# Every second MLP weight chunk split into two parts by DMA instead of by VectorE

## The chip, the cores and the metric

The kernel runs on one core of a Trainium2 chip. The metric is the device time of one execution in microseconds (us); less is better. A core has five engines with instruction queues of their own: TensorE (PE, with its weight loads PEld), VectorE (DVE), ScalarE (ACT), GpSimd (POOL) and SyncE (SP). They meet only at semaphores. DMA transfers are issued from the queues of SP, ACT and POOL and move data between DRAM and the on-chip memory SBUF on 16 DMA engines.

## What is computed

One decoder layer for 256 tokens of width 1024. The input is normalised and projected; attention and a gated recurrence run side by side, are merged and projected back; then comes an MLP. The part that the change touches is the MLP's weights:

```
u = rms_norm(h, mlp_pre_norm[l])
m = jnp.square(jax.nn.relu(u @ w_mlp_up[l])) @ w_mlp_down[l]
h = h + rms_norm(m, mlp_post_norm[l])
```

All products are wanted at nearly float32 accuracy. TensorE works here on a shorter format, float32r, so each float32 operand is split as hi = round(raw) and lo = raw - hi, and each product is made of three: hi by hi, hi by lo, lo by hi.

## The kernel before

All weights lie in DRAM as 74 chunks of 1 MB, each a tile of 128 partitions x 2048 float32, in their order of use. Chunks 0 to 41 belong to the mixer, 42 and 43 to the MLP's first 512 up-projected columns, 44 to 57 (C_UP) to the rest of the up projection, 58 to 73 (C_DN) to the down projection.

For each chunk `load` (L65) takes a buffer `wraw` and lets SP issue the transfer. `split` (L75) then lets ScalarE round the raw tile into `whi` (L89), and VectorE subtract to get `wlo` (L90). For chunks 17 to 22 VectorE does the rounding too (L87). Each of the three kinds of tile has three buffers (L45 to L47), which are reused: a load waits until the split has read the raw buffer, and a split waits until TensorE has finished with the chunk that had its buffers.

`ahead(c)` (L95) is called before and after the products with a chunk and keeps loads three to four chunks and splits one to two chunks in front of the products. Splits are recorded at high priority, so a scheduler moves them forward among the other work of their engine; it also decides which buffer a tile gets. After that each engine runs its instructions strictly in order.

In the up projection (L596 to L616) a chunk takes 16 pairs of matrix products: 512 columns with `whi` (L606), then 256 columns with `wlo` (L607). ScalarE and VectorE then square the result and split it (L608 to L616). In the down projection (L470 to L483, products at L465 to L467) a chunk takes products with `whi`, `wlo` and `whi` again. In both, the second kind of product already needs `wlo`.

At the start, SP issues the input pieces, then chunks 1 and 2 in quarters and 3 in halves (L119 to L121), then the tokens `x_tok` (L124), then the later chunks. ScalarE's sums of squares over `x_tok` (L219) stand ahead of the rounding of chunk 4 in its queue.

Of the kernel before, what the change touches and what calls it, by code (L numbers as in the profile page):

```python
# [9 lines left out]
F32 = mybir.dt.float32  # L10
F32R = mybir.dt.float32r
AF = mybir.ActivationFunctionType
ALU = mybir.AluOpType
PSUM = bass.MemoryType.PSUM

P = 128
T = 256
D = 1024
# [4 lines left out]
MASK_VALUE = -1e30  # L23

# chunks of weights, 1 MB each, in their order of use
# (x_lru and v in turns)
C_XL, C_V, C_Q, C_K, C_RGA, C_RGI = 0, 1, 8, 12, 16, 17
C_GL, C_GA, C_GEL, C_BA, C_BL, C_OUT, C_UPT, C_UP, C_DN = 18, 22, 26, 30, 34, 38, 42, 44, 58
NCHUNK = 74

# the part of a chunk whose upper half is taken by the vector engine instead of the scalar engine
HI_ON_VECTOR = {c: 1.0 for c in range(17, 23)}

# columns of the channel-major parameters (8 columns each)
(P_W0, P_W1, P_W2, P_W3, P_CB, P_BA, P_BI, P_LAM, P_G1, P_G2) = range(0, 80, 8)
# [4 lines left out]
def hybrid_layer(ctx: ExitStack, tc: tile.TileContext, head_d, x_d, w_d, cst_d, gp_d, out_d):  # L40
    nc = tc.nc

    const = ctx.enter_context(tc.tile_pool(name="const", bufs=1))
    slot = ctx.enter_context(tc.tile_pool(name="slot", bufs=1))
    wraw_p = ctx.enter_context(tc.tile_pool(name="wraw", bufs=3))  # L45
    whi_p = ctx.enter_context(tc.tile_pool(name="whi", bufs=3))
    wlo_p = ctx.enter_context(tc.tile_pool(name="wlo", bufs=3))  # L47
# [13 lines left out]

# [1 line left out]
    raws, splits = {}, {}  # L63

    def load(c, parts=1):  # L65
        raw = wraw_p.tile([P, 2048], F32, tag="wraw", name=f"wraw{c}")
        n = 2048 // parts
        for i in range(parts):
            nc.sync.dma_start(raw[:, i * n:(i + 1) * n], w_d[c - 1, :, i * n:(i + 1) * n])
        raws[c] = (raw, parts)  # L70

    # chunks whose parts stay longer lie in tiles that are free by then
    own_slots = {C_OUT + 2: (8, 10), C_OUT + 3: (5, 6)}

    def split(c):  # L75
        raw, parts = raws.pop(c)
        if c in own_slots:
            hi, lo = (slot_tile(i, f"w{c}_{i}", F32R, (P, 2048)) for i in own_slots[c])
        else:
            hi = whi_p.tile([P, 2048], F32R, tag="whi", name=f"whi{c}")  # L80
            lo = wlo_p.tile([P, 2048], F32R, tag="wlo", name=f"wlo{c}")
        n = 2048 // parts
        for i in range(parts):
            s = slice(i * n, (i + 1) * n)
            k = i * n + int(n * HI_ON_VECTOR.get(c, 0))
            if k > i * n:
                nc.vector.tensor_copy(hi[:, i * n:k], raw[:, i * n:k])  # L87
            if k < (i + 1) * n:
                nc.scalar.copy(hi[:, k:(i + 1) * n], raw[:, k:(i + 1) * n])  # L89
            nc.vector.tensor_tensor(lo[:, s], raw[:, s], hi[:, s].bitcast(F32), ALU.subtract)  # L90
        splits[c] = (hi, lo)
# [3 lines left out]
    def ahead(c):  # L95
        """loads and splits that run ahead of the products with chunk c"""
        while state["load"] < min(NCHUNK, c + 4):
            load(state["load"])
            state["load"] += 1
        while state["split"] < min(NCHUNK, c + 2):  # L100
            with tc.high_priority():
                split(state["split"])
            state["split"] += 1

# [1 line left out]
    eps = const.tile([P, 1], F32, name="eps")  # L106
    nc.vector.memset(eps, EPS)
    first = small.tile([P, 1], F32, tag="warm", name="first")
    nc.scalar.copy(first, eps)
    # parameters, then by block of the contraction: x, features on partitions, and chunk 0 of the weights  # L110
    head = const.tile([P, NPAR + 512], F32, name="head")
# [14 lines left out]
    make_identity(nc, ident)  # L126
    # mask[q, 128 + k] = k <= q ? 0 : MASK_VALUE
    mask = const.tile([P, 2 * P], F32, name="mask")
# [21 lines left out]

# [1 line left out]
    def three(out, wh, wl, xh, xl, start, stop):  # L152
# [4 lines left out]
    def first_chunk(xh, xl):  # L157
        """the same, block by block of the contraction, as the operands arrive"""
        hi, lo = splits.pop(0)
        banks = [mm_bank(f"mm0_{o}")[:, 0:T] for o in range(2)]  # L160
        for kb in range(KB):
            for o in range(2):
                s = slice(kb * 256 + o * P, kb * 256 + (o + 1) * P)
                three(banks[o], hi[:, s], lo[:, s], xh[:, kb, :], xl[:, kb, :], kb == 0, kb == KB - 1)
        return banks

    def feat_chunk(c, xh, xl, urgent=False):
        """two blocks of output features, [P features, 2, T]; unless what follows is urgent, the next split precedes it"""
        ahead(c + 1)
        hi, lo = splits.pop(c)  # L170
        hi = hi.rearrange("p (k c) -> p k c", k=KB)
        lo = lo.rearrange("p (k c) -> p k c", k=KB)
        bank = mm_bank(f"mm{c}").rearrange("p (o t) -> p o t", o=2)
        for o in range(2):
            for kb in range(KB):
                s = slice(o * P, (o + 1) * P)
                three(bank[:, o, :], hi[:, kb, s], lo[:, kb, s], xh[:, kb, :], xl[:, kb, :],
                      kb == 0, kb == KB - 1)
        if not urgent:
            ahead(c + 2)  # L180
        return bank

    # x_lru and the causal convolution
    PADW = T + 4
# [4 lines left out]
    xcl = slot_tile(6, "xcl", F32R)  # L189
    # v, tokens on partitions  # L190
    vt = slot.tile([P, 2, D], F32, tag="s11", name="vt")
# [61 lines left out]

    # sp8 = 8 softplus(-lam) = 8 (max(-lam, 0) + log1p(exp(-|lam|))), log1p(z) = 2 atanh(z / (2 + z))
    lam = par[:, P_LAM:P_LAM + 8]
# [23 lines left out]

    # q, k with rotary positions on features 0..31 of each head  # L280
    # (rows 0..31 of all heads are brought together as [4 x 32, 2 heads, T] for it)
    swap = list(range(16, 32)) + list(range(16))
# [19 lines left out]

    # r, i gates
    rt = slot_tile(7, "rt")
# [16 lines left out]

    # RG-LRU: a = exp(-sp8 r), mult^2 = -expm1(-2 sp8 r) = tanh(sp8 r) (1 + a^2)
    mult = slot_tile(3, "mult")
# [25 lines left out]

    # attention, one head in steps  # L350
    ath = slot_tile(12, "ath", F32R)
# [34 lines left out]
    heads = []  # L386
# [8 lines left out]

    # the three gates, with the attention of one head between chunks
    gL = slot_tile(4, "gL")
# [28 lines left out]

    # branch projections; merged = 0.5 (1 + tanh(gL / 2)) y_lru + 0.5 (1 + tanh(gA / 2)) y_attn
    mgh = slot_tile(1, "mgh", F32R)
# [18 lines left out]

# [1 line left out]
    halves = (slice(0, 512), slice(512, 1024))  # L449

    def tok_products(c0, n, act, parts):
        """act(kb) -> (hi, lo) of [P, T]; the last two chunks go one part of the result at a time"""
        acc = [[at_bank(f"acc{c0}_{b}{i}") if i < 2 else mm_bank(f"acc{c0}_{b}{i}") for i in range(len(parts[b]))]
# [31 lines left out]
    class TokenNorm:  # L485
        """1 / sqrt(mean(y^2) + eps) per token, y in parts"""

# [18 lines left out]

    # output projection, post norm, residual; then the next norm's input, features on partitions
    # (both parts of a block side by side, [P, T upper | T lower])
    u2 = [slot_tile(i, f"u2_{i}", F32R, (P, 4, 512)) for i in (12, 3)]
# [36 lines left out]
    def square_of_norm(b):  # L546
        """the norm's factor enters relu(.)^2 as its square, per token, after the down projection"""
        n = TokenNorm("h", 2)
        for i in range(2):
            r2 = n.part(i, x_tok[:, b, halves[i]])  # L550
        nc.vector.tensor_tensor(scl2[:, b:b + 1], r2, r2, ALU.mult)
# [5 lines left out]

# [1 line left out]
    rrh = [slot_tile(i, f"rrh{i}", F32R) for i in (4, 1, 2, 5)]  # L559
    rrl = [slot_tile(i, f"rrl{i}", F32R) for i in (7, 6, 8, 10)]  # L560

    # the first 512 columns with tokens on partitions, one block of tokens at a time
    ahead(C_UPT + 1)
# [69 lines left out]
def _rotary(np):  # L633
    """cosines and signed sines for rows 0..31 of a head, four times over"""
    inv = np.float32(500000.0) ** (-np.arange(0, 32, 2, dtype=np.float32) / np.float32(32))
    ang = (np.arange(T, dtype=np.float32)[:, None] * inv[None, :].astype(np.float32)).T
    cos = np.concatenate([np.cos(ang)] * 2)
    sin = np.concatenate([-np.sin(ang), np.sin(ang)])
    return np.tile(np.stack([cos, sin], axis=1), (4, 1, 1)).astype(np.float32)


def _pack(np, inp):
    """layout only: pieces of the inputs in the order and the form in which the chip reads them"""
    def a(name):
# [70 lines left out]
```

## Time and profile before

| | |
|---|---|
| time, median of 2 runs | 449.38 us (449.33 to 449.43) |
| span of the profiled execution | 447.7 us |
| PE busy | 437.3 us (98%) |
| DVE busy | 302.2 us (67%) |
| ACT busy | 241.0 us (54%) |
| POOL busy | 21.5 us (5%) |
| DMA moved | 83.59 MB, mean 187 GB/s |

The span is what the profiler saw of one execution; the time is 1.7 us longer. A busy share is over the whole span, so it says nothing on which engine ends a given stage; that is read from the waits and from the order in time.

### The profile page before, as it was taken

How to read it: one execution, taken by the hardware profiler on the slowest of the kernel's cores; microseconds unless marked ns; L12 is line 12 of the kernel's file. 1: busy time of each engine (PE TensorE's matmuls, PEld its weight loads, DVE VectorE, ACT ScalarE, POOL GpSimd, SP SyncE). 2: the span in 40 equal slices, each digit the busy share in tenths (PEclk: the TensorE clock that was granted, in tenths of full speed). 3: DMA queues.
4: the chain of work that ended last, by engine and by line, in shares of the span. 5: the costliest groups of instructions: out<-in, count | busy, mean ns of one | idle time of the engine just before them, and what ended most of it. 6: DMA issues, size and time to landing. Idle time of an engine off the chain costs nothing.

```text
span 447.7 us, 7026 instructions
## 1 busy us (share of the span) xinstructions
PE 437.3 (98%) x2916; PEld 402.2 (90%) x2916; DVE 302.2 (67%) x383; ACT 241.0 (54%) x342; POOL 21.5 (5%) x48
## 2 busy tenths in 40 slices
PE   6999999999999999999999999999999999999994
PEld 6999999999999999999998878888888888888884
DVE  5749975779997666885688566777777744444425
ACT  6686743409897575553556475555555433333322
POOL 1000073202000000000000000000000000000000
PEclk9999999999999999999999999999999999999999
DMA  8977555655634356355567703455555545455202
GB/s 269 408 286 284 180 204 206 215 202 194 208 122 167 122 194 233 120 182 189 187 219 258 277 0 132 171 190 184 192 182 188 188 182 192 184 188 193 83 1 94
DMA packets 14575, 83.59 MB, mean 187 GB/s; under 512 B 1808, under 2 KB 2576, under 8 KB 5456
## 3 DMA queue, kind: packets, MB, share of 16 engines
q1 hardware_dynamic: 13520, 80.39, 49.9%
q0 software_dynamic: 736, 2.36, 1.5%
q8 instruction: 23, 0.38, 0.3%
q10 hardware_dynamic: 288, 0.39, 0.2%
q14 instruction: 8, 0.07, 0.0%
HBM read 81.04 MB, written 1.05 MB: 183 GB/s over the span
## 4 chain that ended last, share of the span: by engine, by line
PE 97%; DMA 1%; ACT 0%; DVE 0%; issue 0%; DVEq 0%; ACTq 0%
PE mm L153 14%; PE mm L154 14%; PE mm L155 14%; PE up L606 12%; PE acc L467 8%; PE acc L466 8%; PE acc L465 8%; PE up L607 6%; PE v L204 2%; PE v L203 2%; PE v L202 2%; PE up L574 1%; PE up L572 1%; PE rg L153 1%; PE rg L155 1%; PE rg L154 1%
## 5 line engine op out<-in xcount | busy, mean ns | idle before, releaser
L90 DVE TENSOR_TENSOR wlo<-wraw,whi 128x2048 fp32r<-128x2048 f32 (+2 forms) x78 | 163.6, 2100 | 89.5 <-ACT whi L89 89.3
L89 ACT CAST whi<-wraw 128x2048 fp32r<-128x2048 f32 (+2 forms) x72 | 125.3, 1740 | 127.8 <-PE acc L467 44.4
L153 PE MATMUL mm<-xgh,whi 128*128 128x256 f32 x384 | 109.8, 290 | 4.2 <-ACT xgh L144 4.2
L154 PE MATMUL mm<-xgl,whi 128*128 128x256 f32 x384 | 109.1, 284 | 0.0
L155 PE MATMUL mm<-xgh,wlo 128*128 128x256 f32 x384 | 108.9, 284 | 0.0
L606 PE MATMUL up<-u,whi 128*128 128x512 f32 x224 | 78.9, 396 | 0.0
L153 PEld LDWEIGHTS mm<-xgh,whi 128*128 128x128 f32 x384 | 72.7, 191 | 4.6 <-ACT xgh L144 4.2
L154 PEld LDWEIGHTS mm<-xgl,whi 128*128 128x128 f32 x384 | 73.4, 191 | 0.5
L155 PEld LDWEIGHTS mm<-xgh,wlo 128*128 128x128 f32 x384 | 73.4, 191 | 0.0
L607 PE MATMUL up<-u,wlo 128*128 128x256 f32 x224 | 63.0, 281 | 0.0
L467 PE MATMUL acc<-whi,rrl 128*128 128x512 f32 (+1 forms) x160 | 56.0, 350 | 0.0
L466 PE MATMUL acc<-wlo,rrh 128*128 128x512 f32 (+1 forms) x160 | 55.8, 349 | 0.0
L465 PE MATMUL acc<-whi,rrh 128*128 128x512 f32 (+1 forms) x160 | 55.7, 348 | 0.0
L606 PEld LDWEIGHTS up<-u,whi 128*128 128x128 f32 x224 | 42.1, 188 | 9.9
L607 PEld LDWEIGHTS up<-u,wlo 128*128 128x128 f32 x224 | 42.3, 189 | 0.0
L466 PEld LDWEIGHTS acc<-wlo,rrh 128*128 128x128 f32 x160 | 30.1, 188 | 4.4
L465 PEld LDWEIGHTS acc<-whi,rrh 128*128 128x128 f32 x160 | 30.2, 189 | 4.3
L467 PEld LDWEIGHTS acc<-whi,rrl 128*128 128x128 f32 x160 | 30.1, 188 | 4.1
L153 PE MATMUL mm<-lrh,whi 128*128 128x256 f32 x64 | 18.1, 283 | 0.0
L154 PE MATMUL mm<-lrl,whi 128*128 128x256 f32 x64 | 18.1, 283 | 0.0
L155 PE MATMUL mm<-lrh,wlo 128*128 128x256 f32 x64 | 18.1, 283 | 0.0
L154 PE MATMUL mm<-atl,whi 128*128 128x256 f32 x64 | 18.0, 282 | 0.0
(197 smaller groups left out, 640.8 us busy)
## 6 DMA issues: line engine op xcount, KB each, us to landing
wraw<-in_w_dram SPq DMA_DIRECT2D x70, 1024.0 KB, 4.8
wraw<-in_w_dram SPq DMA_DIRECT2D x8, 256.0 KB, 6.5
xw_a<-in_head_dram SPq DMA_DIRECT2D x4, 256.0 KB, 3.9
wraw<-in_w_dram SPq DMA_DIRECT2D x2, 512.0 KB, 7.0
x_tok<-in_x_dram SPq DMA_DIRECT2D x1, 1024.0 KB, 9.2
gp<-in_gp_dram POOLq DMA_DIRECT2D x1, 1024.0 KB, 4.6
xw_b<-in_head_dram SPq DMA_DIRECT2D x3, 256.0 KB, 4.6
out_dram<-res ACTq DMA_DIRECT2D x2, 192.0 KB, 2.0
```

The lines of the kernel that those rows point to most:

```text
L89: nc.scalar.copy(hi[:, k:(i + 1) * n], raw[:, k:(i + 1) * n])
L90: nc.vector.tensor_tensor(lo[:, s], raw[:, s], hi[:, s].bitcast(F32), ALU.subtract)
L153: nc.tensor.matmul(out, wh, xh, start=start, stop=False)
L154: nc.tensor.matmul(out, wh, xl, start=False, stop=False)
L155: nc.tensor.matmul(out, wl, xh, start=False, stop=stop)
L202: nc.tensor.matmul(banks[b], xgh[:, kb, s], hi[:, k, :], start=kb == 0, stop=False)
L203: nc.tensor.matmul(banks[b], xgh[:, kb, s], lo[:, k, :], start=False, stop=False)
L465: nc.tensor.matmul(out, xh[:, s], hi[:, hs], start=first, stop=False)
L466: nc.tensor.matmul(out, xh[:, s], lo[:, hs], start=False, stop=False)
L467: nc.tensor.matmul(out, xl[:, s], hi[:, hs], start=False, stop=last)
L606: nc.tensor.matmul(bank, hi[:, kb, c], u2[kb // 4][:, kb % 4, :], start=kb == 0, stop=False)
L607: nc.tensor.matmul(bank[:, 0:T], lo[:, kb, c], u2h(kb, slice(0, T)), start=False, stop=kb == KB - 1)
```

## The change

In the MLP's chunks 44, 46, ... 72 (every second one, 15 in all) neither SP loads a raw tile nor VectorE subtracts. Instead POOL issues two transfers for each:

1. `load`: a transfer from DRAM, float32, straight into a `whi` tile of type float32r. The transfer rounds.
2. `split`: ScalarE writes -hi into the `wlo` tile (an activation with scale -1, in place of the rounding); then POOL issues a second transfer of the same 1 MB, which adds the raw weights to what lies in `wlo`.

The odd chunks stay as they were. The `wraw` tiles have two buffers now instead of three, `whi` four instead of three, for the whole kernel. Comments and docstrings went as well, which shifts line numbers.

```diff
-    wraw_p = ctx.enter_context(tc.tile_pool(name="wraw", bufs=3))
-    whi_p = ctx.enter_context(tc.tile_pool(name="whi", bufs=3))
+    wraw_p = ctx.enter_context(tc.tile_pool(name="wraw", bufs=2))
+    whi_p = ctx.enter_context(tc.tile_pool(name="whi", bufs=4))
...
+    BY_DMA = set(range(C_UP, NCHUNK, 2))
+
     def load(c, parts=1):
+        if c in BY_DMA:
+            hi = whi_p.tile([P, 2048], F32R, tag="whi", name=f"whi{c}")
+            nc.gpsimd.dma_start(hi, w_d[c - 1])
+            raws[c] = (hi, 0)
+            return
...
     def split(c):
         raw, parts = raws.pop(c)
+        if c in BY_DMA:
+            lo = wlo_p.tile([P, 2048], F32R, tag="wlo", name=f"wlo{c}")
+            nc.scalar.activation(lo, raw.bitcast(F32), AF.Copy, scale=-1.0)
+            nc.gpsimd.dma_start(lo, w_d[c - 1], accum_op=ALU.add)
+            splits[c] = (raw, lo)
+            return
```

POOL's queue in the MLP was empty before; its last row was the transfer of the gains `gp`. Now it holds this (`whi54` is chunk 54's rounded tile, L71 the rounding load, L88 the adding load):

```order
L88 DMA wlo50_3169<-in_w_dram 128x2048
L71 DMA whi54_3264<-in_w_dram 128x2048
L88 DMA wlo52_3266<-in_w_dram 128x2048
L71 DMA whi56_3361<-in_w_dram 128x2048
L88 DMA wlo54_3363<-in_w_dram 128x2048
```

So the adding load of chunk 52 stands behind the rounding load of chunk 54, and so on in pairs. By the semaphores in the built program, the load of `whi54` waits for TensorE's last product with chunk 49, whose buffer it takes; the pattern holds from there to the end, `whi` of c + 4 after the products of c - 1.

ScalarE's queue at the same place, before (`rl` is the up projection's copy at L608, `rrh` the rounded activation at L615):

```order
L89 CAST whi53_3319<-wraw53_3219 128x2048
L615 CAST rrh1_2833<-rv_3226 128x512
L608 COPY rl_3274<-up_6_1_3295 128x256
L608 COPY rl_3323<-up_7_0_3325 128x256
L89 CAST whi54_3368<-wraw54_3268 128x2048
```

and now:

```order
L103 CAST whi53_3314<-wraw53_3215 128x2048
L622 COPY rl_3269<-up_6_1_3290 128x256
L622 COPY rl_3318<-up_7_0_3320 128x256
L629 CAST rrh2_2834<-rv_3270 128x512
L87 ACTIVATE wlo54_3363<-whi54_3264 128x2048
```

The negation stands where the rounding of the even chunk stood, with the small `rrh` now ahead of it. It waits for its `whi` to land and for the last product with chunk 51, whose `wlo` buffer it takes.

VectorE's queue early in the kernel, where only the number of raw buffers changed, before (`xc` and `xlp` belong to the convolution, `mm4` is the result of chunk 4's products):

```order
L90 TENSOR_TENSOR wlo5_328<-wraw5_218,whi5_327 128x2048
L246 SCALAR_TENSOR_TENSOR xc_160<-xlp_158,head_86,xc_160 128x256 x2
L90 TENSOR_TENSOR wlo6_397<-wraw6_270,whi6_396 128x2048
L246 SCALAR_TENSOR_TENSOR xc_160<-xlp_158,head_86,xc_160 128x256 x3
L90 TENSOR_TENSOR wlo7_452<-wraw7_325,whi7_451 128x2048
```

and now:

```order
L104 TENSOR_TENSOR wlo5_328<-wraw5_218,whi5_327 128x2048
L260 SCALAR_TENSOR_TENSOR xc_160<-xlp_158,head_86,xc_160 128x256 x6
L255 TENSOR_TENSOR xlp_158<-mm2_276,rstd_365 128x2x256
L255 TENSOR_TENSOR xlp_158<-mm4_400,rstd_365 128x2x256
L104 TENSOR_TENSOR wlo6_397<-wraw6_270,whi6_396 128x2048
```

The subtraction for chunk 6 has moved behind the use of chunk 4's result. On SP, chunk 3's load now waits for the split of chunk 1, and the load of `x_tok` stands behind it as before; chunk 4's load waits for the split of chunk 2 instead of that of chunk 1.

## Rows read from the trace of the kernel before

**Rows 1.** The page, parts 1 and 4: busy time, and the chain that ended last.

```profile
PE 437.3 (98%) x2916; PEld 402.2 (90%) x2916; DVE 302.2 (67%) x383; ACT 241.0 (54%) x342; POOL 21.5 (5%) x48
...
PE 97%; DMA 1%; ACT 0%; DVE 0%; issue 0%; DVEq 0%; ACTq 0%
```

**Rows 2.** Windows, mostly the up projection: busy us per engine, clock, DMA share, GB/s.

```profile
265.00:360.00 95.00, 94.93 (x531) 81.96 (x530) 67.37 (x84) 52.65 (x71) 0.00 (x0) 1.00 0.50 176
```

**Rows 3.** Timeline, up projection: start us, us, instruction, idle before and its releaser.

```profile
318.23 1.91 ACT L89 CAST whi<-wraw 128x2048 fp32r<-128x2048 f32 x1 [2.36 <-PE up L606]
...
320.18 2.29 DVE L90 TENSOR_TENSOR wlo<-wraw,whi 128x2048 fp32r<-128x2048 f32 x1 [1.47 <-ACT whi L89]
...
322.50 5.96 SPq L69 DMA_DIRECT2D wraw<-in_w_dram  x2
...
323.65 0.68 DVE L614 SCALAR_TENSOR_TENSOR rv<-rl 128x512 f32<-128x512 f32 x1
...
323.86 1.91 ACT L89 CAST whi<-wraw 128x2048 fp32r<-128x2048 f32 x1 [2.36 <-PE up L606]
```

**Rows 4.** Timeline, down projection.

```profile
380.17 1.91 ACT L89 CAST whi<-wraw 128x2048 fp32r<-128x2048 f32 x1 [3.71 <-PE acc L467]
...
385.79 1.91 ACT L89 CAST whi<-wraw 128x2048 fp32r<-128x2048 f32 x1 [3.71 <-PE acc L467]
```

**Rows 5.** Windows of 1 us across the load issued at 322.50.

```profile
323.40:324.40 1.00, 1.00 (x8) 0.87 (x7) 0.93 (x3) 0.54 (x1) 0.00 (x0) 1.00 0.80 180
324.40:325.40 1.00, 1.00 (x8) 0.86 (x7) 0.00 (x0) 1.00 (x1) 0.00 (x0) 1.00 0.97 393
325.40:326.40 1.00, 1.00 (x7) 0.91 (x6) 0.60 (x1) 1.00 (x3) 0.00 (x0) 1.00 0.96 401
326.40:327.40 1.00, 1.00 (x7) 0.88 (x6) 1.00 (x1) 0.53 (x2) 0.00 (x0) 1.00 0.18 74
```

**Rows 6.** DMA issues: tile, queue, count, KB each, median us from issue to landing.

```profile
wraw<-in_w_dram SPq DMA_DIRECT2D x70, 1024.0 KB, 4.8
...
gp<-in_gp_dram POOLq DMA_DIRECT2D x1, 1024.0 KB, 4.6
```

**Rows 7.** The issue of `gp` on POOL: ns, start us.

```profile
L446 POOL DMA_DIRECT2D gp<-in_gp_dram x1: 550/550/550, 165.8 to 165.8; - x1
```

**Rows 8.** Windows: `gp` and a load from SP in flight together.

```profile
166.00:167.00 1.00, 1.00 (x11) 1.00 (x10) 0.93 (x1) 1.00 (x4) 0.40 (x1) 1.00 0.00 0
167.00:168.00 1.00, 1.00 (x11) 1.00 (x10) 1.00 (x1) 0.20 (x1) 0.00 (x0) 1.00 0.92 377
...
167.20:172.40 5.20, 5.20 (x45) 5.15 (x44) 2.87 (x7) 2.89 (x8) 0.00 (x0) 1.00 0.98 380
```

**Rows 9.** Timeline where the up projection begins.

```profile
272.94 1.91 ACT L89 CAST whi<-wraw 128x2048 fp32r<-128x2048 f32 x1 [0.89 <-PE up L574]
274.75 0.59 ACT L576 ACTIVATE upt<-up 128x512 f32<-128x512 f32 x1
...
278.69 0.48 PE L606 MATMUL up<-u,whi 128*128 128x512 f32 x1
```

**Rows 10.** Timeline of the start: SP's issues, chunk 4's split, its first product with `wlo`.

```profile
11.98 0.38 SPq L124 DMA_DIRECT2D x_tok<-in_x_dram  x1
...
14.03 7.23 SPq L69 DMA_DIRECT2D wraw<-in_w_dram  x3
...
21.16 1.06 ACT L219 ACTIVATE junk<-x_tok 128x1024 f32<-128x1024 f32 x1 [1.51 <-DMA x_tok<-in_x_dram]
...
25.25 1.91 ACT L89 CAST whi<-wraw 128x2048 fp32r<-128x2048 f32 x1 [0.16 <-DMA wraw<-in_w_dram]
...
27.20 2.29 DVE L90 TENSOR_TENSOR wlo<-wraw,whi 128x2048 fp32r<-128x2048 f32 x1 [1.90 <-ACT whi L89]
...
29.95 0.28 PE L155 MATMUL mm<-xgh,wlo 128*128 128x256 f32 x1
```

**Rows 11.** DMA throughput from 8 to 26 us in 40 slices.

```profile
GB/s 214 137 209 259 341 396 387 392 364 405 428 423 369 382 405 419 401 410 419 410 391 410 419 419 410 428 401 492 401 437 382 401 437 346 492 346 510 364 455 419
```

## The prediction

> **What bounds the kernel now.** I read the busy shares and the chain of work that ended last [rows 1]: TensorE is busy 437.3 of 447.7 us, and 97% of the chain is its own work. So it waits for almost nothing, and the 10.4 us in which it is idle lie at the start and behind the last product. In the stage that the change touches first it is full as well (94.93 of 95 us), while VectorE and ScalarE have room and the DMA engines are half busy [rows 2]. Work taken from VectorE therefore buys nothing; what is left to find is whether the new way of making `wlo` is in time.
>
> For that I read the order in time. ScalarE's roundings of `whi` begin when TensorE releases a buffer, at 318.23 and 323.86 [rows 3], in the down projection at 380.17 and 385.79 [rows 4]: TensorE takes 5.63 us per chunk, 11.26 per pair. Rounding takes 1.91 us and the subtraction 2.29, back to back, so `wlo` is there 4.3 us after the release (320.18 + 2.29 - 318.23 = 4.24). The release is the end of the products with chunk c - 1, and `wlo` of c + 2 is used after those with c and c + 1, 11.26 us later. The old way has 7 us to spare. The new way must fit its two transfers into the same 11.26 us.
>
> **What the change takes away.** 15 subtractions of 2.29 us on VectorE, 34 us: worth nothing, since no wait of TensorE hangs on them. 15 plain loads from SP. On ScalarE the negation takes the place of the rounding; the same tile and the same kind of operation, so 1.91 us each, no change.
>
> **What it adds, timed from s, the end of the products with chunk c - 1 (c even).** By the order, the rounding load of c + 4 and the negation for c + 2 are both let go at s; the adding load of c + 2 stands on POOL behind that rounding load and waits for the negation.
>
> - The rounding load. The trace has no load that changes the type. The nearest row is `gp`: 1 MB from POOL's queue, 4.6 us from issue to landing [rows 6], 0.55 us of POOL [rows 7], first bytes about 1.2 us after the issue (165.8 to just after 167.0 [rows 8]). A plain load from SP is alike: 4.8 us, of which the DMA engines work 0.80 + 0.97 + 0.96 + 0.18 = 2.9 [rows 5]. I take the rate of two transfers in flight together, 380 GB/s at 98% busy [rows 8]: 2.76 us per MB. Bounds: 2.76, and twice that, 5.5, if rounding halves the rate.
> - The negation is let go at s, but `rrh` is now ahead of it. `rrh` needs VectorE's squaring (L614), which ends 6.1 us after the chunk before is through (323.65 + 0.68 - 318.23 [rows 3]), that is at s + 0.5, and takes some 0.6 us itself (as `upt` [rows 9]). The negation then runs from s + 1.1 to s + 3.0; the adding load could have first bytes at about s + 4.3.
> - The adding load. The trace has none. It has to read 1 MB from DRAM and 1 MB of `wlo`. Lower bound: a plain load, 2.76 us. Upper bound: three times that, 8.3, if reading, adding and writing don't overlap. I take two times, 5.5, by the row in which 2 MB are moved at 380 GB/s, because two operands must come in.
> - The odd chunk's plain load falls into the same stretch. Its raw buffer is released when VectorE has subtracted, 4.3 us after the end of chunk c, that is s + 9.9, so by the next pair's clock at s - 1.3; it works on the engines from s - 0.2 to s + 2.8, beside the rounding load that begins at s + 1.3.
>
> Sum: at s + 1.3 the plain load has 1.45 us left, the rounding load needs 2.76, the adding load 5.5 behind it in the same queue: data complete at s + 11.0, and about 0.7 for the landing (the last bytes at 326.6, landing at 322.5 + 4.8 = 327.3 [rows 5, 6]): s + 11.7. TensorE wants it at s + 11.26, or some 0.2 later, since one product with `whi` goes ahead. Late by 0.2 to 0.4. Since the next pair was issued before that delay arose, a late pair gives the following one as much more time, and the mean loss is half: 0.1 to 0.2 us. DMA work per pair is 2.9 + 2.76 + 5.5 = 11.2 us of 11.26: it fits, with nothing to spare, so I count 0.15 us for each of the 13 chunks 48 to 72: 2 us. If adding costs no more than a plain load, data are there at s + 9.0 and the sum is zero.
>
> The Trainium skill has a rule on this (Collectives: The Full Stack, section "The bandwidth ceiling: the fold count and why AG ≠ RS ≠ AR"): an adding transfer is slower than a copy not through the addition but through its two source reads, which share one ring, and runs at about half the rate of a copy. By a plain load's row the sum would be 0, by this rule 2 us; no run here shows an adding load yet.
>
> The first pair is special. Chunk 46's negation stands on ScalarE behind the rounding of chunk 45, which can start at 272.94 at the earliest, and `upt` (0.59 us) [rows 9]: 272.94 + 1.91 + 0.59 + 1.91 = 277.35. The adding load then lands at 277.4 + 1.2 + 5.5 + 0.7 = 284.8. Chunk 45 starts at 278.69, chunk 46 so at 284.3 and its first `wlo` product 0.2 later [rows 9, 3]: 0.3 us late.
>
> **Two raw buffers instead of three**, for all 44 chunks ahead of the MLP. A raw buffer is held for a load (4.8 us), a rounding (1.91) and a subtraction (2.29), together 9.0 us; two of them give a chunk every 4.5 us, against 5.63 that TensorE takes. So it holds once it runs. At the start it is tight: chunk 4's subtraction ends at 27.20 + 2.29 = 29.49, and TensorE wants it at 29.95 [rows 10]. Its chain is the load of `x_tok` (landed at 21.16), the sums of squares, the rounding, the subtraction. Now chunk 3's load waits for chunk 1's split, which ends at 14.0 (chunk 4's load waited for the same and went at 14.03, 2 us after `x_tok` at 11.98 [rows 10]), and `x_tok` stands behind it. But the DMA engines had a backlog in any case, moving about 400 GB/s from 10 us on [rows 11], and what stood ahead of chunk 3 is all but through by then; the gap I estimate at half a microsecond. Loss 0.3 us; bounds 0 and 3, the whole delay of the issue with its 1 MB.
>
> **Sum.** 447.7 + 0.3 + 0.3 + 2 = 450.3 us of span; the time lies 1.7 us above the span, so 452.0.
>
> **Rivals.**
>
> 1. DMA becomes the bound (slower). For it: no row shows either kind of load, and my sum leaves no slack, so any further cost shows at once. If rounding halves the rate too, a pair needs 2.9 + 5.5 + 5.5 = 13.9 us of DMA work, 2.6 over: 13 pairs x 2.6 = 34 on top of 450, 484 us. With three times for the adding load and a plain rate for rounding it is 2.9 + 2.76 + 8.3 = 14.0, the same price. With both, 16.7 and +71, 521 us. It decides once rounding and adding load together take over 9.0 us (11.26 + 0.6 a pair is the 2%, less 2.9). Against it: `gp` shows that POOL's queue as such is not slower than SP's.
> 2. The front starves with two raw buffers. Chunk 6's subtraction now stands on VectorE behind the use of chunk 4's result, and each load two subtractions back. For it: chunk 4 has 0.46 us of slack. Against: 4.5 us against 5.63 per chunk, so it can fall behind only where VectorE's queue is late as well. Price: 0 to 3 us for each of some three chunks until it has caught up, up to 9; it ends at 452 to 461.
> 3. It does not matter at all, or helps: adding costs as much as a plain load, and VectorE's 34 us let something start sooner. TensorE's idle 10.4 us are the first 4 us before any operand is there and the last 6 behind the last product, which the change does not reach. 449 to 450 us; a gain of 2% is all but excluded.
>
> **How the numbers follow.** My forecast (adding at half rate, rounding at full rate, no visible loss) 0.45; rival 1 0.42, of which 0.17 for its dear end; rival 2 0.09, half of it over 2%; rival 3 0.04. A change of about 2% is what a measurement of this kernel can tell from none, 440 to 458 us. Within it: 0.45 + 0.045 + 0.02, less 0.02 for a forecast that runs over; I say 0.49. Slower 0.49, faster 0.02. The likeliest case alone lies at 449 to 458; the range reaches to the cheap end of rival 1 with some margin, 449 to 492, and leaves out its dear end.
>
> **What would show it.** In the changed kernel: 15 rounding and 15 adding loads on POOL; landing 5 to 7 us after the issue for the rounding loads, and under 9 for the adding ones; DMA share near 1.0 and not 0.50 in the two MLP stages; waits of TensorE's `up` and `acc` products for the DMA of `wlo` of under 3 us in total. Step by step: if the adding load alone takes over 8 us on the engines, or the rounding load over 5, the price of rival 1 is right, with waits of 2 us and more before every even chunk and the time near 484. If TensorE waits before 60 us, it is rival 2. My prediction is wrong in its premise if the waits stand elsewhere: on ScalarE's negation, or on odd chunks whose plain load came late.

## The result and the profile after

The changed kernel takes 474.99 us (474.40 to 475.57) against 449.38 before: a ratio of 1.0564, 95% interval 1.0525 to 1.0603. It is slower by 5.6%. Run again beside later experiments it took 474.68 us, ratio 1.0575 (1.0547 to 1.0602). The profiled execution has a span of 473.8 us, 26.1 more than before.

Parts 1 and 4 of the page, the answer to [rows 1]:

```profile
PE 443.3 (94%) x2916; PEld 404.0 (85%) x2916; DVE 268.7 (57%) x368; ACT 242.3 (51%) x342; POOL 43.4 (9%) x78
...
PE 46%; issue 35%; DMA 9%; POOL 4%; DVE 4%; ACT 1%; SPq 0%; POOLq 0%; DVEq 0%; ACTq 0%
```

VectorE has lost its 34 us, and nothing came of it. The 35% "issue" of the chain is time for which the profile shows no releaser, so I go by the list of waits instead. TensorE's busy time has grown by 6 us although it does the same 2916 products, in part because some ran at a lower clock. The rest of the 26 us is idle time, and the list of waits (us in total, times, longest) names the releaser of the larger part:

```profile
PEld acc L480 <- DMA wlo<-in_w_dram: 9.9, 6, 2.4
PEld up L621 <- DMA wlo<-in_w_dram: 8.5, 4, 4.2
PE acc L480 <- DMA wlo<-in_w_dram: 7.9, 5, 2.1
PE up L621 <- DMA wlo<-in_w_dram: 7.2, 4, 3.9
```

The `PE` rows are the products that wait, 7.9 + 7.2 = 15.1 us; the `PEld` rows are their weight loads, the same waits seen once more. Part 6 of the page has the transfers (KB each, median us from issue to landing), beside 4.8 for a plain load in [rows 6]:

```profile
wraw<-in_w_dram SPq DMA_DIRECT2D x55, 1024.0 KB, 5.0
whi<-in_w_dram POOLq DMA_DIRECT2D x15, 1024.0 KB, 7.8
wlo<-in_w_dram POOLq DMA_DIRECT2D x15, 1024.0 KB, 11.0
```

In windows (columns as in [rows 2]) the DMA share over the up projection is 0.83 instead of 0.50 there. The second row is a stretch of it behind the longest wait, with the clock at 0.52:

```profile
266.00:370.00 104.00, 94.92 (x514) 80.70 (x513) 52.91 (x83) 54.37 (x82) 10.48 (x15) 0.98 0.83 226
...
294.50:298.00 3.50, 3.50 (x12) 3.02 (x13) 0.00 (x0) 0.00 (x0) 0.00 (x0) 0.52 1.07 417
```

The timeline of TensorE shows that wait and what follows it; a product with 512 columns takes 0.63 us where it takes 0.40 elsewhere:

```profile
294.48 0.44 PE L621 MATMUL up<-u,wlo 128*128 128x256 f32 x1 [3.89 <-DMA wlo<-in_w_dram]
294.71 0.63 PE L620 MATMUL up<-u,whi 128*128 128x512 f32 x1
```

**Where the 26.1 us are.** The first product of `up` with chunk 44 starts at 278.56 instead of 272.73: 5.8 us are lost ahead of the MLP. From there to the end of the span it is 195.2 us instead of 175.0: 20.3 us are lost in the MLP, 15.1 of them waits for `wlo`, about 3.2 two stretches at near half clock of 3.5 us each (the other begins at 369.5); the rest, some 2 us, I can't place. I call these two numbers the front loss and the MLP loss and give them for every kernel below. Of one kernel below, that with three raw buffers, two of the four executions took 467.8 and 468.3 us at a granted clock of 0.99, against 459.9 and 461.0 at 1.00; its trace and its time are of the latter two.

### The profile page after: what moved, and what is told of

The parts are those of the page before. It is cut to its first block, busy times and chain, and to the rows that moved or that the text cites. A ratio compares the mean times of both kernels' runs of the same rounds, so it can differ in the third digit from the quotient of the medians.

```text
span 473.8 us, 7067 instructions
## 1 busy us (share of the span) xinstructions
PE 443.3 (94%) x2916; PEld 404.0 (85%) x2916; DVE 268.7 (57%) x368; ACT 242.3 (51%) x342; POOL 43.4 (9%) x78
## 3 DMA queue, kind: packets, MB, share of 16 engines
q1 hardware_dynamic: 11360, 64.66, 38.0%
q0 software_dynamic: 5056, 33.82, 29.1%
## 4 chain that ended last, share of the span: by engine, by line
PE 46%; issue 35%; DMA 9%; POOL 4%; DVE 4%; ACT 1%; SPq 0%; POOLq 0%; DVEq 0%; ACTq 0%
PE mm L169 10%; PE mm L168 9%; PE mm L167 9%; PE acc L480 3%; PE acc L481 3%; PE acc L479 3%; DMA wlo<-in_w_dram 2%; POOL wlo L88 2%; DMA x_tok<-in_x_dram 2%; DVE wlo L104 2%; POOL whi L71 1%; DMA wraw<-in_w_dram 1%; DMA rot<-qT 1%; DMA xw_a<-in_head_dram 1%; PE up L586 1%
## 5 line engine op out<-in xcount | busy, mean ns | idle before, releaser
L104 DVE TENSOR_TENSOR wlo<-wraw,whi 128x2048 fp32r<-128x2048 f32 (+2 forms) x63 | 129.2, 2053 | 119.1 <-ACT whi L103 99.1
L103 ACT CAST whi<-wraw 128x2048 fp32r<-128x2048 f32 (+2 forms) x57 | 96.7, 1696 | 99.2 <-DMA wraw<-in_w_dram 48.4
L620 PE MATMUL up<-u,whi 128*128 128x512 f32 x224 | 80.3, 401 | 0.0
L621 PE MATMUL up<-u,wlo 128*128 128x256 f32 x224 | 64.0, 286 | 7.2 <-DMA wlo<-in_w_dram 7.2
L480 PE MATMUL acc<-wlo,rrh 128*128 128x512 f32 (+1 forms) x160 | 57.0, 356 | 8.0 <-DMA wlo<-in_w_dram 7.9
L87 ACT ACTIVATE wlo<-whi 128x2048 fp32r<-128x2048 f32 x15 | 28.7, 1911 | 21.3 <-PE acc L480 21.3
L71 POOL DMA_DIRECT2D whi<-in_w_dram x15 | 8.2, 543 | 207.3 <-PE mm L169 64.7
L623 DVE TENSOR_TENSOR rl<-up,rl 128x256 f32<-128x256 f32 x28 | 11.3, 420 | 20.2 <-ACT rl L622 20.2
L629 ACT CAST rrh<-rv 128x512 fp32r<-128x512 f32 x14 | 8.7, 620 | 22.4 <-DVE rv L628 22.4
```

Of the source, the lines that this page charges most:

```text
L71: nc.gpsimd.dma_start(hi, w_d[c - 1])
L87: nc.scalar.activation(lo, raw.bitcast(F32), AF.Copy, scale=-1.0)
L480: nc.tensor.matmul(out, xh[:, s], lo[:, hs], start=False, stop=False)
L620: nc.tensor.matmul(bank, hi[:, kb, c], u2[kb // 4][:, kb % 4, :], start=kb == 0, stop=False)
L621: nc.tensor.matmul(bank[:, 0:T], lo[:, kb, c], u2h(kb, slice(0, T)), start=False, stop=kb == KB - 1)
```

## Experiments

Line numbers shift from kernel to kernel. Here are the first trace and all twelve runs after it; the times are medians of four executions (of two for the first trace and for the kernel with three raw buffers), the two losses (us) are read from the one execution that was traced.

| kernel | time | front loss | MLP loss |
|---|---|---|---|
| changed kernel, first trace | 474.99 | 5.8 | 20.3 |
| changed kernel, repeated | 474.68 | 7.5 | 17.8 |
| buffer counts only | 454.17 | 5.5 | 0.1 |
| buffer counts, `x_tok` moved | 451.37 | 1.8 | -0.1 |
| three raw buffers ahead of the MLP | 460.5 | 0.1 | 11.4 |
| second transfer adds nothing | 455.97 | 6.0 | -0.4 |
| every fourth chunk | 456.43 | 5.2 | 2.5 |
| quarter of the odd loads | 464.69 | 6.0 | 7.5 |
| `wlo` tiles of its own, adding load earlier | 489.24 | 14.8 | 24.3 |
| rounding load earlier | 466.85 | 7.3 | 10.7 |
| quarter and rounding load earlier | 459.66 | 5.8 | 4.0 |
| changed kernel, `x_tok` moved | 473.60 | 7.8 | 18.3 |
| changed kernel without chunk 46 | 467.31 | 3.2 | 14.7 |

### The two parts of the loss apart

The buffer counts alone:

```diff
-    BY_DMA = set(range(C_UP, NCHUNK, 2))
+    BY_DMA = set()
```

> Only the buffer counts of the change (two raw, four rounded); every chunk is still loaded plainly and split by ScalarE and VectorE. Theory: the 5.8 us by which the changed kernel starts its up projection later come from the two raw buffers alone, through VectorE's and ScalarE's queues, so this kernel takes 449.4 + 5.8 = 455.2 us (454 to 457), with the first product of the up projection at about 278.5 instead of 272.7 and no wait of TensorE in the MLP. Rival: the early loss needs something else of the change (the transfers on GpSimd, or the order of ScalarE's queue around chunk 44); then 449 to 451 us.

454.17 us, ratio 1.0105 (1.0074 to 1.0135). `up` starts at 278.27 and TensorE waits for nothing in the MLP: as the theory said. But the 5.5 us are made up differently. There are two waits, 1.82 at 31.58 and 1.73 at 122.18, and a fall of the clock behind the first. In windows:

```profile
32.00:36.00 4.00, 4.00 (x23) 4.00 (x22) 4.00 (x7) 1.24 (x3) 0.00 (x0) 0.57 0.87 279
```

The changed kernel has the clock at 1.00 there, but a third wait, below. That the sums agree is partly chance.

The other way round, one buffer serving as raw until chunk 43 and as `whi` from chunk 44 on:

```diff
+    def raw_tile(c):
+        k = c % 3 if c < C_UP else (c // 2) % 2
+        return w_p.tile([P, 2048], F32, tag=f"w{k}", name=f"wraw{c}")
+    def hi_tag(c):
+        if c < C_UP:
+            return 3 + c % 3
+        return hi_tag(c - 3) if c % 2 else 2 if c == C_UP else hi_tag(c - 5)
```

> The MLP split by DMA as in the changed kernel, but ahead of the MLP three raw and three rounded buffers as before; one of the raw buffers becomes the fourth rounded one at chunk 44. Theory: the two losses are independent and add up; 475.0 - 5.8 = 469.2 us (467 to 471), up projection starting at about 273, waits of TensorE for the DMA of wlo as in the changed kernel, some 15 us. Rival: the early loss is swallowed or called forth by what follows (a later start gives the MLP's loads a head start); then 472 to 476 us here.

459.9 and 461.0 us, below both expectations. `up` starts at 272.86, so the front loss is gone. The MLP loss is 11.4 us, not 20: the waits for `wlo` are 5.1 + 3.7 us, that in front of chunk 46 is 1.7 instead of 3.9, and the clock stays up. In these two executions the losses don't simply add. Two are little to go by: whether the MLP loss is as small whenever the third raw buffer is there stays open. That the front loss comes with the two raw buffers does not hang on it.

### What makes `wlo` late

The second transfer without its addition:

```diff
-            nc.gpsimd.dma_start(lo, w_d[c - 1], accum_op=ALU.add)
+            nc.gpsimd.dma_start(lo, w_d[c - 1])
```

> The changed kernel, but the second transfer is a plain rounding load into wlo and adds nothing: the low parts of the even MLP chunks are left out (they hold the rounded weights). Same queue, same waits, same bytes from DRAM. Theory: the loss in the MLP hangs on the adding load's half rate (629 ns for a packet of 8 KB against 325 of the rounding load); at full rate wlo lands 2.5 us and more earlier, and the rounding load behind it too, so that TensorE waits for wlo under 2 us in total: 455 to 458 us, the early loss alone. Rival: what is late is the chain of two issues, two first bytes and a negation, whatever the rate; then wlo lands at best 1 us earlier and 465 us or more remain.

455.97 us, ratio 1.0136 (1.0121 to 1.0152), no wait for `wlo`. The chain of issues is the same, so the adding load's rate is a necessary part of the MLP loss. (The packet times in the expectation are those of the trace's packet records.) The queue rows in part 3 of the pages (packets, MB, share of 16 engines over the span) give each transfer's price. Of the changed kernel, and of this one:

```profile
q1 hardware_dynamic: 11360, 64.66, 38.0%
q0 software_dynamic: 5056, 33.82, 29.1%
```

```profile
q0 software_dynamic: 5056, 33.82, 20.7%
```

q0 is POOL's queue. Before, it had 1.5% of 447.7 us, 6.7 us. In the changed kernel 29.1% of 473.8 is 137.9, less 6.7 over 15 chunks 8.75 us for a rounding and an adding load. Here 20.7% of 453.3 is 93.8, less 6.7 over 30 loads 2.90 for a rounding one. So an adding load takes 5.84, twice as much. q1, SP's queue, has 180 us for 64.66 MB, 2.92 per chunk. A pair's DMA work is 8.75 + 2.92 = 11.7 us, and TensorE takes 11.26 for it. The Trainium skill (Collectives: The Full Stack, section "The bandwidth ceiling: the fold count and why AG ≠ RS ≠ AR") has, for collectives, the reducing transfer at about half the rate of the copying one, because it reads two sources. The trace agrees on the rate for a load, 5.84 against 2.90 us; no run here shows the reason.

Half as many chunks by DMA:

```diff
-    BY_DMA = set(range(C_UP, NCHUNK, 2))
+    BY_DMA = set(range(C_UP, NCHUNK, 4))
```

> The changed kernel, but only every fourth MLP chunk (44, 48, ... 72) is split by DMA. A round of rounding load, negation and adding load, some 13.3 us from release to landing, then has 22.5 us of TensorE's products to hide behind. Theory: no wait for wlo is left, and the time is that of the two raw buffers alone, 454 to 456 us. Rival: each of the late rounds costs something of its own wherever it stands (a transfer of 1 MB that pushes aside the plain loads of the neighbouring chunks); then half of the MLP's loss remains, 463 to 466 us.

456.43 us, ratio 1.0141 (1.0121 to 1.0162). Four waits of some 0.45 us are left, where none was expected. The timelines of POOL and TensorE show one, with no other transfer in the queue ahead:

```profile
316.96 0.86 POOL L88 DMA_DIRECT2D wlo<-in_w_dram  x1 [20.86 <-ACT wlo L87]
```

```profile
324.97 0.39 PE L621 MATMUL up<-u,wlo 128*128 128x256 f32 x1 [0.46 <-DMA wlo<-in_w_dram]
```

The adding load takes 8.0 us from issue to use, in all of this kernel's rounds but the first, whose load falls ahead of the MLP (10.8). So does the last one of the changed kernel, issued at 446.42 with no other load in flight; the engines work 0.72 of these 8.0 us, 5.8:

```profile
446.42:454.42 8.00, 8.00 (x43) 6.82 (x42) 2.29 (x1) 1.50 (x1) 0.87 (x1) 1.00 0.72 131
```

In the kernel with every fourth chunk the negation stands behind a rounding on ScalarE and the issue comes 4.1 us after the release; in the changed kernel it comes after 2.4 (1.8 in the down projection, which has no `rrh` ahead of the negation). So even with free engines the chain takes 2.4 + 8.0 = 10.4 us of 11.26. The changed kernel's chain for one pair, POOL first:

```profile
331.58 0.54 POOL L71 DMA_DIRECT2D whi<-in_w_dram  x1 [9.60 <-PE up L621]
334.02 0.88 POOL L88 DMA_DIRECT2D wlo<-in_w_dram  x1 [1.89 <-ACT rl L622]
```

```profile
344.13 0.39 PE L621 MATMUL up<-u,wlo 128*128 128x256 f32 x1 [1.30 <-DMA wlo<-in_w_dram]
```

Release at 331.58, adding load issued 2.4 us later, usable 10.1 us after that, 2.1 more than with every fourth chunk. There the rounding load comes behind the adding load; in the changed kernel it is in front of it, and lands at 339.2.

Next, less DMA work, with the chain as it is:

```diff
+        if c > C_UP:
+            nc.sync.dma_start(raw[:, 0:512], w_d[c - 1, :, 0:512])
+            raws[c] = (raw, parts)
+            return
```

> The changed kernel, but of the odd MLP chunks only the first quarter is loaded (256 KB) and used four times over; three quarters of their weights are left out. ScalarE and VectorE do as much as before. Theory: the term that was too small is the rounding load, which took 7.5 to 9.8 us instead of 5.0 because it shares the engines with the odd chunk's plain load and the tail of the adding load; without 2.2 us of that work it lands at 5 to 6 us, wlo 11.3 us or less after the release, and the waits for wlo are under 3 us in total: 455 to 459 us. Rival: the length lies in GpSimd's queue itself (issue, first bytes, one transfer behind the other), whatever else the engines do; then rounding loads still take over 7 us and 468 us or more remain.

464.69 us, ratio 1.0336 (1.0293 to 1.0379): between the two. In the up projection rounding loads land in 5.0 to 6.7 us, but the adding loads still take 8.0 and 9.4 by turns (up to 7.2 and 10.6 in the down projection), and 6.2 us of waits remain. Relieving the engines takes away 12.8 of 20.3 us, not all.

Then the chain shortened, with the DMA work as it is. The first attempt gave `wlo` of the even chunks its own tiles:

```diff
-            lo = wlo_p.tile([P, 2048], F32R, tag="wlo", name=f"wlo{c}")
+            lo = slot_tile((0, 11)[c // 2 % 2], f"wlo{c}", F32R, (P, 2048))
```

> The changed kernel, but wlo of the even MLP chunks lies in two tiles that are free by then, so the negation need not wait for TensorE's last product with chunk c - 1: by the order it stands ahead of it, and on GpSimd the adding load of c + 2 now ahead of the rounding load of c + 4. The same transfers. Theory: the DMA engines can do a pair's work in 11.26 us; the loss in the MLP is a chain that starts too late (rounding load, then adding load, both after s). With the adding load let go 3 to 4 us earlier, waits for wlo are under 2 us in total: 455 to 459 us, the early loss alone. Rival: the engines' rate is the limit (2.9 + 2.8 + 5.5 us and more of a pair of 11.26); then an earlier issue only lengthens the queue, and 466 to 475 us remain.

489.24 us, ratio 1.0881 (1.0863 to 1.0899), slower by far, and neither theory's number. Of the 13.0 us by which its span is longer than the changed kernel's, 9.0 are lost ahead of the MLP and 4.0 in it. The timelines of ScalarE and POOL show why, first ahead of the MLP, then in it:

```profile
263.71 1.91 ACT L87 ACTIVATE wlo<-whi 128x2048 fp32r<-128x2048 f32 x1 [8.21 <-DMA whi<-in_w_dram]
265.52 0.58 ACT L510 ACTIVATE junk<-acc 128x512 f32<-128x512 f32 x1
```

```profile
336.30 1.91 ACT L87 ACTIVATE wlo<-whi 128x2048 fp32r<-128x2048 f32 x1 [4.07 <-DMA whi<-in_w_dram]
...
338.51 0.88 POOL L88 DMA_DIRECT2D wlo<-in_w_dram  x1 [11.37 <-ACT rl L622]
...
339.07 0.87 POOL L71 DMA_DIRECT2D whi<-in_w_dram  x1
```

Chunk 46's rounding load, issued right behind chunk 44's adding load at 246.7, takes 17.0 us to land; the negation waits for it, and the squares of the norm (L510) and with them the MLP wait behind the negation. In the MLP too a rounding load now stands behind the adding load before it on POOL (issues 338.51 and 339.07), lands 10.0 us later, the negation waits for it, and only then is the next adding load issued: a ring of 0.6 + 10.0 + 1.9 + 0.3 = 12.8 us that paces the up projection (12.7 to 16.9 from issue to issue in the down projection). While the negation waits, ScalarE's other work waits behind it. So this run does not tell the two theories apart.

The second attempt was to take the rounding load out of the chain, with two more tiles for `whi`:

```diff
-            hi = whi_p.tile([P, 2048], F32R, tag="whi", name=f"whi{c}")
+            own = {0: 0, 2: 11}.get(c // 2 % 4)
+            if own is None:
+                hi = whi_p.tile([P, 2048], F32R, tag="whi", name=f"whi{c}")
+            else:
+                hi = slot_tile(own, f"whi{c}", F32R, (P, 2048))
```

> The changed kernel with two more tiles for whi of the even MLP chunks (free by then), so that the rounding load of c + 4 is let go earlier and stands on GpSimd ahead of the adding load of c instead of c + 2. The same transfers and bytes; the negation and the adding load still start at s. Theory: a pair's DMA work, 11.3 us by the kernel with three raw buffers (94% of a period of 12.0), just fits, and the loss is a chain that starts too late; with the rounding load out of the chain wlo lands some 10 to 11 us after s and the waits are under 4 us in total: 456 to 460 us. Rival: the engines cannot be kept full to more than 94%, so the period stays at 12.0 us, 0.75 us per pair and some 10 us in all: 464 to 468 us, more where TensorE's clock falls after a wait.

466.85 us, ratio 1.0385 (1.0337 to 1.0434), the rival's number. In windows the engines are close to full, and TensorE has 75.58 of 79 us; the changed kernel in the same window stands below it:

```profile
286.00:365.00 79.00, 75.58 (x419) 65.15 (x418) 43.22 (x60) 39.73 (x53) 9.02 (x13) 0.98 0.96 264
```

```profile
286.00:365.00 79.00, 71.80 (x397) 61.79 (x396) 40.24 (x56) 38.47 (x52) 8.51 (x12) 0.98 0.94 253
```

But the edit did half of what it was for. On POOL the rounding loads now come in twos:

```profile
330.11 0.55 POOL L75 DMA_DIRECT2D whi<-in_w_dram  x1 [7.06 <-PE up L625]
332.19 0.87 POOL L92 DMA_DIRECT2D wlo<-in_w_dram  x1 [1.53 <-ACT rl L626]
335.99 0.55 POOL L75 DMA_DIRECT2D whi<-in_w_dram  x1 [2.93 <-PE up L625]
345.40 0.88 POOL L92 DMA_DIRECT2D wlo<-in_w_dram  x1 [8.86 <-ACT rl L626]
```

Only every second adding load has lost the rounding load just ahead of it: that of 345.40 takes 7.9 us, that of 332.19 takes 10.3. Of the 8.0 us of waits for `wlo` 7.2 stand behind loads of the latter kind. So the run gives the rival's number without showing the rival's reason: what remains may be DMA's rate or the half of the chain that was left. Both reliefs at once:

> Both reliefs at once: of the odd MLP chunks only the first quarter is loaded (three quarters of their weights are left out), and the rounding loads are let go earlier into two more tiles. Theory: the loss in the MLP has two parts, the DMA work of a pair (11.3 us of 11.26) and the chain from the release over negation and adding load (10.4 us alone, 8.0 of it the adding load); either relief alone left half of it (7.5 and 10.7 us of 20.2), both together leave the first stall at chunk 46 and hardly another, 0 to 3 us: 456 to 459 us with the early loss. Rival: something third (TensorE's clock after a wait, ScalarE's order) holds the rest; then 463 us or more.

459.66 us, ratio 1.0228 (1.0210 to 1.0247); the MLP loss is 4.0 us against 0 to 3 expected, with waits for `wlo` of 2.8 in all. The window has the engines at 0.78 and TensorE at 79.02 of 80:

```profile
292.00:372.00 80.00, 79.02 (x443) 68.07 (x442) 42.60 (x58) 42.35 (x54) 9.38 (x13) 1.00 0.78 196
```

The two reliefs together take away all of the MLP loss but 4 us: 20.3 without them (17.8 in the repeated run), 10.7 and 7.5 with one, 4.0 with both. So both the DMA work and the chain have a part in it. How large each part is by itself these runs don't tell, since neither relief was complete and less DMA work also lets the chain's loads land sooner.

### The front, and chunk 46

`x_tok` ahead of chunk 3 on SP's queue, first in the kernel with the buffer counts alone:

```diff
     load(2, 4)
+    x_tok = slot.tile([P, 2, D], F32, tag="xtok", name="x_tok")
+    nc.sync.dma_start(x_tok, x_d.rearrange("(b p) d -> p b d", p=P))
     load(3, 2)
```

> The kernel that has only the buffer counts of the change (454.2 us), with the load of x_tok moved on SyncE's queue ahead of chunk 3's two halves, which now wait for a raw buffer. Theory: the first of its two waits, 1.83 us ahead of chunk 4's wlo products at 31.58, comes from x_tok standing behind that wait (sums of squares, rounding and subtraction of chunk 4 in one line), and TensorE's clock is at half for the 4 us behind it; both go, 3.5 us: 450 to 451.5 us. Rival: chunk 4's raw buffer itself is late, or chunk 3 now is; then a wait before 35 us remains and 453 us or more.

451.37 us, ratio 1.0039 (1.0024 to 1.0054): the wait at 31.58 is gone and the clock stays up, 2.8 us in all. The wait near 120 is still there, 1.26 us. The missing wait alone would prove little: of the ten traces with two raw buffers and `x_tok` in its old place, three (second transfer adds nothing, quarter of the odd loads, `wlo` tiles of its own) have no such wait either; ScalarE starts on `x_tok` at 21.9 to 22.6 there and at 22.8 to 23.9 in the other seven. The times, at most 451.5 against at least 453.2 us, are the better witness, though from two chips.

> The changed kernel with one move: the load of x_tok ahead of chunk 3's on SyncE's queue. Theory: its first wait, 1.71 us ahead of 31.27, goes as it did in the kernel with the buffer counts alone (where the time fell by 2.8 us, a stretch at half clock included, which the changed kernel does not have there); the rest stays: 472 to 474 us. Rival: an earlier start of 1.7 us is eaten up at the later waits of the front (119.85 and 261.57), which hang on transfers; then 475 us.

473.60 us (471.3 to 475.6), against 474.68 (474.5 to 477.1) of the changed kernel on the same chip. The first wait went here too, but that near 120 grew to 2.0 us, with the clock at 0.59 in the 4 us behind it; `up` starts no earlier, at 280.56. The trace is of the slowest of the four executions. A gain can't be told from this.

The changed kernel again, to see whether the quicker transfers of the kernel with three raw buffers were the chip's:

> The changed kernel itself once more, beside the others of this group. With three raw buffers ahead of the MLP its transfers landed faster (rounding loads 7.4 us in the middle against 7.8, adding loads 10.1 against 11.0), which the buffers do not explain. If this differs from chip to chip, the time here may lie 2 to 5 us lower, at 470 to 473 us; if not, at 474 to 476 us.

474.68 us, with the same 3.9 us in front of chunk 46: the first measurement was no outlier. But this run and that with three raw buffers were on different chips, so whether the quicker transfers were the chip's stays open.

The front loss is 7.5 us here and 5.8 in the first trace. The waits ahead of the MLP are alike (1.71, 1.0 and 2.21 us against 1.71, 1.31 and 2.30), but behind the third the clock fell in this trace and not in the first, here in this order:

```profile
262.50:266.00 3.50, 3.50 (x11) 2.98 (x12) 2.70 (x9) 2.17 (x8) 0.00 (x0) 0.54 1.04 246
```

```profile
262.50:266.00 3.50, 3.50 (x18) 2.88 (x17) 2.45 (x9) 2.17 (x9) 0.00 (x0) 1.00 1.03 253
```

So differences of some 2 us between the losses of two traces can be the clock's.

Chunk 46 alone split the old way:

```diff
-    BY_DMA = set(range(C_UP, NCHUNK, 2))
+    BY_DMA = set(range(C_UP, NCHUNK, 2)) - {C_UP + 2}
```

> The changed kernel, but chunk 46 alone is split the old way again. Theory: the wait of 3.9 us for its wlo and the stretch of 3.5 us behind it with TensorE's clock near half (products of 0.63 instead of 0.40 us, some 1.6 us lost) both go, and nothing takes their place: 474.7 - 5.5 = 469.2 us (468.5 to 471). Rival: the wait only moves on to chunk 48, whose transfers stood behind it so far; then 473 us or more.

467.31 us, ratio 1.0409 (1.0381 to 1.0437), 2 us better than expected. The wait of 3.9 and the stretch at low clock are gone; in the same window as above the clock is 1.00 and 22 instead of 12 products are through:

```profile
294.50:298.00 3.50, 3.50 (x22) 3.05 (x21) 2.76 (x3) 1.34 (x3) 0.00 (x0) 1.00 1.01 208
```

Another 2.3 us come from ahead of the MLP. ScalarE's timeline of the changed kernel there:

```profile
254.93 1.91 ACT L103 CAST whi<-wraw 128x2048 fp32r<-128x2048 f32 x1 [7.87 <-DMA wraw<-in_w_dram]
256.75 1.91 ACT L87 ACTIVATE wlo<-whi 128x2048 fp32r<-128x2048 f32 x1
258.56 0.58 ACT L510 ACTIVATE junk<-acc 128x512 f32<-128x512 f32 x1
```

and TensorE's:

```profile
261.57 0.63 PE L550 MATMUL hT<-ident,x_tok 128*128 128x128 f32 x4 [2.30 <-issue]
```

The raw chunk lands late; the rounding, the negation for chunk 44 and the squares of the norm stand in line behind it, and `x_tok` and the transposes (L550) wait for the norm; the profile names no releaser here, I read this from the order. Without chunk 46's rounding load that raw chunk lands in time for a rounding at 252.27, and the wait is gone.

## Why the prediction failed where it did

It said 452.0 us, with a range from 449 to 492, and gave slower by over 2% the chance 0.49. The time came out at 475.0, inside the range and between the likeliest case (452) and rival 1 (484). That the range holds it is partly luck: it reached so far for the sake of a dearer load, which did not come, and 5.8 of the 26.1 us are lost ahead of the MLP, where the sum had 0.3. Step by step:

- **TensorE bounds the kernel, VectorE's relief is worth nothing:** right.
- **The transfers' prices** were nearly right: rounding 2.90 us (2.76 taken), adding 5.84 (5.5), plain 2.92 (2.9). But the sum was put at 11.2 of 11.26 "with nothing to spare", and the small errors, all of one sign, make it 11.7. That alone is 0.4 x 13 = 5 us, where I counted 2. By the bound that I gave rival 1, 9.0 us for both loads, 8.75 would still be within 2%; that bound counted the engines' work alone.
- **The chain is the term that was mis-sized.** Predicted: adding load issued at s + 3.1, landed at s + 11.7. Measured: issued at s + 2.4 (s + 1.8 in the down projection; `rrh`, ahead of the negation, is through at s + 0.2 and not s + 1.1), but 10.1 to 12.7 us in flight instead of 8.6, so there at s + 12.5 to s + 14.5, 13.2 in the mean. Alone it takes 8.0, not 1.2 + 5.5 + 0.7 = 7.4; the rest is sharing. By my sum the rounding load is through at s + 5.5 and landed at s + 6.2; from 307 us on it lands 7.4 to 9.8 us after its issue. One reason stands in the times: a late adding load of the pair before is still on the engines at s (it lands at 344.13, and the next rounding load was issued at 342.8). I had only the other side of that, the halving.
- **That halving,** (L' - 11.26) / 2 a pair, fits roughly: with the L' = 13.2 measured it gives 1.0 us, 12.6 for 13 chunks, and the waits behind the first are 11.2 us in all.
- **Chunk 46:** 0.3 us predicted, 3.9 measured, and 1.6 of clock behind it. ScalarE's order was as said, only 5.6 us later with the front (negation through at 282.97 instead of 277.35); the load took 11.2 us instead of 7.4, with a plain load issued at 283.0 beside it.
- **Two raw buffers:** 0.3 us predicted within 0 to 3, and rival 2 at 3 and more: the changed kernel waits 1.71 at 31.27 and 1.31 at 119.85. The first is the place that I named: `x_tok` is issued at 14.68 instead of 11.98 [rows 10], and ScalarE starts on it at 23.15 instead of 21.16. I took half a microsecond for a delay that was 2.0 here (0.7 to 2.7 over the ten traces), on the argument that a backlog on the engines hides it. The second I did not foresee; it is there, 1.0 to 2.0 us, in every trace with two raw buffers, and not in that with three. Its releaser is a transfer of the rotated `kT`; which move of VectorE's queue makes that late was not tried.
- **The third front wait** (2.30) needs the two raw buffers and an early rounding load together: it is absent with three raw buffers, with the buffer counts alone, with every fourth chunk, and without chunk 46. No step of mine had the rounding loads of chunks 44 and 46 delaying the plain loads before the MLP.
- **Rival 1** named the right place but for a wrong reason: neither load is much dearer than forecast. Work that just fits by its sum still waits, because it can't start before its release.

Open: 1.2 of the 4.0 us of MLP loss that remain with both reliefs. The other 2.8 are waits for `wlo`, 1.5 of them behind adding loads that have nothing ahead and take 8.0 us, but are issued some 4 us after the release, as in the kernel with every fourth chunk.

## What to carry to other kernels

A transfer that adds took the DMA engines as long as two loads here, in exchange for work of an engine that nobody waited for; count the DMA work per period first, and where it fills the period take it for a loss. Then lay the chain from the release of a buffer to the use as if the engines were free, and add what shares them: here both had a part, and easing either one left about half of the loss. A buffer taken away also delays the transfers queued behind the load that now waits, as `x_tok` was here.

## What was not expected of the hardware

- After some short waits TensorE's granted clock was near the lower of its two levels, 1.2 of 2.4 GHz: 0.52 in the 3.5 us behind 3.89 idle ones, 0.57 in the 4 us behind 1.82. It stayed at 1.00 behind the 1.71 us at 31.27, and in the kernel with earlier rounding loads behind 2.92 us at 415.28. At one and the same place in two executions of the changed kernel it stayed up behind 2.30 us and fell to 0.54 behind 2.21. Such a stretch cost some 1.6 us more than the wait; which waits bring it on these runs don't tell.
- POOL took 0.87 us to issue an adding load and 0.55 for a rounding one; but a rounding load issued right behind an adding one (339.07, in the kernel with `wlo` tiles of its own) took 0.87 as well.
